# Three of four feed-forward layers of a diffusion backbone: two plain inner tiles in place of four, the gate halves of two more multiplied while the tokens arrive, and joins of fast products made in PSUM

## The chip, the cores and the metric

The kernel runs on one core of a Trainium2 chip. The metric is the device time in microseconds of one execution, the median of several runs. Times below are of that core.

## The reference, cut to what matters

One inference step of a small flow-matching backbone over 640 tokens (512 latent, 128 context) of width 1024. Two layers, each a half-step feed-forward, a token mixer and another half-step feed-forward, so six sub-layers n = 0 to 5: feed-forward at n = 0, 2, 3, 5, a Fourier mixer at n = 1, attention at n = 4.

```python
def _modulation(cond, w_mod, b_mod):
    m = jax.nn.silu(cond) @ w_mod + b_mod
    return m.reshape(cond.shape[0], N_MOD, D_MODEL)

def _swiglu(h, w1, w2):
    gate, up = jnp.split(h @ w1, 2, axis=-1)
    return (jax.nn.silu(gate) * up) @ w2

def _half_ffn(x, m, k, g_pre, g_post, w1, w2):
    h = _modulated_prenorm(x, g_pre, m, k)
    return x + 0.5 * m[:, 3 * k + 2, None] * _rmsnorm(_swiglu(h, w1, w2), g_post)
```

The inner width is 2816, that is 22 inner tiles f of 128. Everything is float32.

## The kernel before, in words

**Arithmetic.** A float32 operand is kept as two parts, hi (a copy on ScalarE in a shorter format, L220) and lo (the remainder, a subtraction on VectorE, L221). A product is three matmuls, hi·hi, hi·lo and lo·hi (`mm3`, L231, lines L234, L235, L236). The 640 tokens are two halves of 320 columns (five tiles of 128 tokens). A weight unit is 128 x 1024: a load of 512 KB into one of four raw buffers (`NRAW` L40, `raw_tile` L170), then its hi and lo. `unit(i)` (L175) sends units up to three ahead of the one that is multiplied; a raw buffer is free again when the last reader of what lies in it is done, and only then can the next load into it begin. Loads stand in one queue of SyncE, in program order.

**First matrix of a feed-forward (w1).** A plain inner tile multiplies gate and up for both halves: 2 x 2 x 8 x 3 = 96 matmuls of 128 x 320. A fast tile (`w1_fast`, L704) takes seven products of four chunks in place of eight, 84 matmuls, and joins them. It needs sums of weights (`send`, L182: gate, then on VectorE three sums at L195 to L197 from gate and up into a buffer `sums`, and a fourth at L203 for the last product, "all") and differences of token halves, made once per layer by `combine` (L666, subtractions at L692). Until those are ready the layer multiplies plain tiles: f = 0 to 3 are plain, 4 to 21 are fast, in each of the four layers. The joins of a fast tile are seven VectorE operations between PSUM banks and temporaries (L715, L718, L722, L728, L729, L733, L735) and three ScalarE ones. Its banks are x and y (kind `score`), z (kind `turn`, one bank) and w (kind `sum`, one bank). x takes the gate products, z and w take two products each, with a join between.

**Second matrix (w2).** After f = 4, 8, 12 and 16 (`SLICES`, L42) the hidden tiles made so far are multiplied with their rows of w2, for all five token tiles, in 512-column matmuls into the four `main` banks.

**Work put behind.** The modulation vectors of later sub-layers are matrix-vector products, done on VectorE: a job loads 512 KB of `w_mod_t` into a raw buffer and runs two SCALAR_TENSOR_TENSORs over it (`gemv`, L427, at L429). `BEHIND` (L44) and `behind` (L213) put nine jobs into each of the slices 0 to 3 of layers n = 0, 2 and 3, two into those of n = 5, and twelve into the Fourier mixer. Each engine runs its instructions in the order of the built program. In that order the nine jobs of a slice stand ahead of the weight sums of the next fast tile but one: after f = 4 and slice 0, the products of f = 5 find their sums ready, and those of f = 6 wait behind the jobs.

**Around it.** At the end of a layer each token tile is normalised and transposed for the next (`chain`, L564, a delay at L602 and transposes at L605). Gate vectors of the post-norm are transposed to rows by `gate_rows` (L531, a PE transpose at L538, its copy at L540), for n and, in layers 0 and 3, also for n + 1, right after each other before f = 20. `plan_ffn` (L819) writes the order of a layer out; the same plan serves all four.

Of the kernel before, what the change touches and what calls it, by code (L numbers as in the profile page):

```python
# [27 lines left out]
NF = DFF // P  # L28
# [14 lines left out]
FAST = range(4, NF)  # L43
# [83 lines left out]
class Kernel:  # L127
# [54 lines left out]
    def send(self, kind, src):  # L182

        nc, two, one = self.nc, slice(512, UNIT), slice(0, 512)
        at = slice(0, UNIT)
        if kind in ("plain", "block", "gate"):
            raw = self.raw_tile(src)  # L190
            self.fast["gate"] = raw
        elif kind == "sums":
            up, gate = self.raw_tile(src), self.fast["gate"]
            raw = self.raw.tile([P, UNIT], F32, tag="raw", name=self.name("sums"))
            nc.vector.tensor_tensor(raw[:, one], gate[:, one], up[:, one], op=ALU.add)  # L195
            nc.vector.tensor_tensor(up[:, one], up[:, one], up[:, two], op=ALU.add)
            nc.vector.tensor_tensor(raw[:, two], gate[:, one], up[:, one], op=ALU.add)  # L197
# [12 lines left out]
        self.split(hi, lo, raw[:, at])  # L210
        return hi, lo
# [352 lines left out]
    def chain(self, n, i, pss, acc=()):  # L564
# [36 lines left out]
        yield {0: 10500, 1: 14000, 2: 9200, 3: 11000, 4: 15000}[i]  # L601
# [19 lines left out]
    def ffn(self, layer, which, base, boundary):  # L621
# [3 lines left out]
        n = layer * 3 + 2 * which  # L625
        begun = [False, False]
# [7 lines left out]
        def w1(fs, half):  # L634
# [4 lines left out]
            if n == half == 0 and 0 in fs:  # L639
                rest, pss = self.begun  # L640
                for go in rest:
                    go()
            elif len(fs) == 1:
                for f in fs:
                    for j in range(2):
                        with self.behind_of(*[] if n or half else (*self.entered, self.load)):
                            w = self.unit(base + self.w1_at[f] + j)
                        with self.tc.issue_after(self.latest.ins):
                            pss.append(self.proj(w, lambda k: k * P, half, kind="score" if f == 2 and n == 0 else "main"))
            else:  # L650
                pss = self.multi([self.unit(base + self.w1_at[f] + j) for f in fs for j in range(2)], half,
                                 ("main", "main", "turn", "sum"))
# [45 lines left out]
        def product(f, ps, unit, at, x, start):  # L698
            w = self.unit(base + self.w1_at[f] + unit)
# [4 lines left out]
        def w1_fast(f):  # L704

            g[f] = self.ring(F32R).rearrange("p (a t) -> p a t", a=2)
            a, q = (self.temp("left")[:, :HALF] for _ in range(2))
            s, v = (self.temp("right")[:, :HALF] for _ in range(2))
            x, y, z = (self.bank(kind)[:, :HALF] for kind in ("score", "score", "turn"))
            product(f, x, 0, 0, lambda k: self.h.chunk(k, 0), True)  # L710
            with high():
                nc.scalar.activation(a, x, AF.Copy)
            product(f, y, 1, 512, lambda k: part(2, k), True)
            with high():
                tt(q, y, a, op=ALU.subtract)  # L715
            product(f, z, 1, 0, lambda k: part(3, k), True)
            with high():
                tt(a, q, z, op=ALU.subtract)  # L718
            w = self.bank("sum")[:, :HALF]
            product(f, w, 2, 0, lambda k: part(1, k), True)  # L720
            with high():
                tt(a, a, w, op=ALU.add)  # L722
            product(f, x, 0, 512, lambda k: self.h.chunk(4 + k, 0), False)
            with high():
                nc.scalar.activation(s, x, AF.Silu)
            product(f, z, 2, 512, lambda k: part(4, k), False)
# [4 lines left out]
            product(f, w, 3, 0, lambda k: self.h.chunk(4 + k, 1), False)  # L731
# [26 lines left out]
        def w2(s, tiles):  # L758
# [7 lines left out]
            for a0, f in [(a, f) for a in range(2) for f in range(f0, f1)] if ends else [(None, f) for f in range(f0, f1)]:  # L766
                w = self.unit(base + self.w2_at[s] + f - f0)
# [20 lines left out]
        for op, a, half in self.ffn_plan:  # L788
# [7 lines left out]
            elif op == "combine":  # L796
                combine(a)
            elif op == "fast":
                w1_fast(a)
# [19 lines left out]
    def plan_ffn(self):  # L819

        plan = []
        for half in (0, 1):
            for i, fs in enumerate(((0, 1), (2,), (3,))):
                plan += [("w1", fs, half)]
                if half:
                    plan += [("combine", step, None) for step in ((), (0, 1), (2, 3))[i]]
        due = 0
        for f in FAST:
            if f == NF - 2:
                plan += [("gates", None, None)]  # L830
            plan += [("fast", f, None)]
# [5 lines left out]
        self.ffn_plan = plan  # L837
        self.ffn_units, self.w1_at, self.w2_at = [], {}, {}
        for op, v, half in plan:
            if op == "fast":  # L840
                self.w1_at[v] = len(self.ffn_units)
                self.ffn_units += [("gate", v, 0), ("sums", v, 1)]
                self.ffn_units += [(kind, None, None) for kind in ("up", "all")]
            elif op == "w1":
                for f in v:
                    if f not in self.w1_at:
                        self.w1_at[f] = len(self.ffn_units)
                        self.ffn_units += [("w1", f, 0), ("w1", f, 1)]
            elif op == "w2" and v[0] not in self.w2_at:
                self.w2_at[v[0]] = len(self.ffn_units)  # L850
                f0, f1 = SLICES[v[0]]
                self.ffn_units += [("w2", f0, j) for j in range(f1 - f0)]

    def list_units(self):
        io = self.io
        self.plan_ffn()
        self.bases = []
        for i in range(DEPTH):
            for sub in range(3):
                self.bases.append(len(self.units))  # L860
                if sub != 1:
                    for op, v, j in self.ffn_units:
                        if op == "w2":
                            self.units.append(("plain", io["w2"][i, sub // 2, v + j]))
                        elif op == "w1":
                            self.units.append(("block" if v == 3 else "plain", io["w1"][i, sub // 2, v, j]))
                        else:
                            self.units.append((op, None if v is None else io["w1"][i, sub // 2, v, j]))
# [598 lines left out]
```

## Time and profile before

| | |
|---|---|
| median of 3 runs | 2233.11 us (2232.19 to 2233.71) |
| profiled execution | 2233.16 us, span 2231.4 us |
| granted TensorE clock in it | 0.996 |
| instructions in the span | 35240 |

The profile comes from one execution on the chip. A row of a group gives the line of the kernel, the engine, the operation, output and input by program name, the count, the busy time, the mean of one and the idle time before it with what ended it. A row of the timeline gives start, duration, engine, line, operation and, in brackets, the idle time before it and its releaser. In the timeline a duration is longer than the distance to the next start, since neighbours overlap by some tenths of a microsecond. In the view by windows each row is a stretch of time: busy time and count of PE, weight loads, VectorE, ScalarE and GpSimd, the granted clock (1.00 is full speed), the DMA share and GB/s.

### The profile page before, as it was taken

How to read it: one execution, taken by the hardware profiler on the slowest of the kernel's cores; microseconds unless marked ns; L12 is line 12 of the kernel's file. 1: busy time of each engine (PE TensorE's matmuls, PEld its weight loads, DVE VectorE, ACT ScalarE, POOL GpSimd, SP SyncE). 2: the span in 40 equal slices, each digit the busy share in tenths (PEclk: the TensorE clock that was granted, in tenths of full speed). 3: DMA queues.
4: the chain of work that ended last, by engine and by line, in shares of the span. 5: the costliest groups of instructions: out<-in, count | busy, mean ns of one | idle time of the engine just before them, and what ended most of it. 6: DMA issues, size and time to landing. Idle time of an engine off the chain costs nothing. (4 is left out here: it accounts for less than half of the span.)

```text
span 2231.4 us, 35240 instructions
## 1 busy us (share of the span) xinstructions
PE 2198.5 (99%) x13730; PEld 2051.7 (92%) x13730; DVE 1682.5 (75%) x3081; ACT 1155.6 (52%) x2186; POOL 43.7 (2%) x95
## 2 busy tenths in 40 slices
PE   7999999999999999999999999999999999999998
PEld 5999999999899999998999999989999899999997
DVE  5888898687868898887688898776555666766684
ACT  4544454464544454455444554466878644455452
POOL 0000000010000000001000000000000000000000
PEclk8999999999999999999999999999999999999999
DMA  8144444432413444444144344523343322322232
GB/s 313 67 142 161 140 143 144 178 127 94 167 72 123 139 146 149 154 143 178 57 143 150 133 147 150 195 77 105 108 118 111 106 74 95 114 87 88 101 123 104
DMA packets 84424, 288.13 MB, mean 129 GB/s; under 512 B 9537, under 2 KB 14497, under 8 KB 84129
## 3 DMA queue, kind: packets, MB, share of 16 engines
q1 hardware_dynamic: 83712, 285.23, 37.6%
q8 instruction: 107, 1.75, 0.3%
q10 hardware_dynamic: 544, 0.66, 0.1%
q14 instruction: 61, 0.49, 0.1%
HBM read 270.34 MB, written 11.58 MB: 126 GB/s over the span
## 5 line engine op out<-in xcount | busy, mean ns | idle before, releaser
L220 ACT ACTIVATE hi<-raw 128x1024 fp32r<-128x1024 f32 (+1 forms) x374 | 358.4, 973 | 330.2 <-PE score L235 86.9
L221 DVE TENSOR_TENSOR lo<-raw,hi 128x1024 fp32r<-128x1024 f32 (+1 forms) x374 | 416.0, 1118 | 142.1 <-ACT hi L220 140.9
L234 PE MATMUL main<-hi,ring 128*128 128x512 f32 (+2 forms) x1044 | 391.4, 375 | 0.0
L235 PE MATMUL main<-lo,ring 128*128 128x512 f32 (+2 forms) x1044 | 387.8, 372 | 0.8 <-DVE lo L221 0.8
L236 PE MATMUL main<-hi,ring 128*128 128x512 f32 (+2 forms) x1044 | 387.2, 371 | 0.0
L429 DVE SCALAR_TENSOR_TENSOR junk<-raw,wide 128x1024 bf16<-128x1024 f32 x256 | 313.1, 1223 | 95.7 <-DMA raw<-in_w_mod_t 91.3
L236 PE MATMUL score<-ring,lo 128*128 128x320 f32 x896 | 277.1, 309 | 0.3 <-DVE lo L221 0.3
L234 PE MATMUL score<-ring,hi 128*128 128x320 f32 x896 | 277.4, 310 | 0.0
L235 PE MATMUL score<-ring,hi 128*128 128x320 f32 x896 | 276.9, 309 | 0.0
L234 PEld LDWEIGHTS main<-hi,ring 128*128 128x128 f32 x1044 | 196.3, 188 | 34.9 <-issue 1.7
L235 PEld LDWEIGHTS main<-lo,ring 128*128 128x128 f32 x1044 | 196.3, 188 | 33.8 <-DVE lo L221 1.1
L236 PEld LDWEIGHTS main<-hi,ring 128*128 128x128 f32 x1044 | 196.1, 188 | 33.9 <-issue 0.2
L234 PE MATMUL turn<-ring,hi 128*128 128x320 f32 x648 | 200.5, 309 | 2.3 <-DVE left L718 2.1
L236 PE MATMUL sum<-ring,lo 128*128 128x320 f32 x648 | 200.2, 309 | 0.0
L235 PE MATMUL sum<-ring,hi 128*128 128x320 f32 x648 | 200.2, 309 | 0.0
L234 PE MATMUL sum<-ring,hi 128*128 128x320 f32 x648 | 200.2, 309 | 0.0
L235 PE MATMUL turn<-ring,hi 128*128 128x320 f32 x648 | 200.2, 309 | 0.0
L236 PE MATMUL turn<-ring,lo 128*128 128x320 f32 x648 | 200.2, 309 | 0.0
L781 ACT ACTIVATE y<-main 128x512 f32<-128x512 f32 x160 | 94.2, 591 | 200.0 <-PE main L236 199.0
L234 PE MATMUL main<-ring,hi 128*128 128x320 f32 x560 | 181.8, 325 | 1.6 <-ACT ring L220 1.6
L235 PE MATMUL main<-ring,hi 128*128 128x320 f32 x560 | 174.9, 312 | 0.8 <-DVE ring L221 0.8
L236 PE MATMUL main<-ring,lo 128*128 128x320 f32 x560 | 174.8, 312 | 0.0
(247 smaller groups left out, 4371.4 us busy)
## 6 DMA issues: line engine op xcount, KB each, us to landing
raw<-in_w SPq DMA_DIRECT2D x264, 512.0 KB, 3.9
raw<-in_w_mod_t SPq DMA_DIRECT2D x128, 512.0 KB, 3.5
raw<-in_qkv SPq DMA_DIRECT2D x26, 512.0 KB, 3.8
first<-in_w_mod_k SPq DMA_DIRECT2D x16, 512.0 KB, 8.8
spill<-ring SPq DMA_DIRECT2D x12, 640.0 KB, 2.9
ring<-spill SPq DMA_DIRECT2D x12, 640.0 KB, 7.2
raw<-in_bias SPq DMA_DIRECT2D x16, 448.0 KB, 3.8
raw<-in_four_in SPq DMA_DIRECT2D x8, 512.0 KB, 3.8
```

The costliest lines, as they stand in the source:

```text
L220: a = self.nc.scalar.activation(hi, src, AF.Copy)
L221: self.last_split = a, self.nc.vector.tensor_tensor(lo, src, hi.bitcast(F32), op=ALU.subtract)
L234: mm(out, whi, xhi, start=start, stop=False)
L235: mm(out, whi, xlo, start=False, stop=False)
L236: self.latest = mm(out, wlo, xhi, start=False, stop=stop)
L429: last = self.nc.vector.scalar_tensor_tensor(out=self.junk, in0=raw, scalar=1.0, in1=self.wide[:, cond, :], op0=ALU.mult, op1=ALU.mult, ac ...
L781: nc.scalar.activation(place(i, a), ps[a], AF.Copy)
```

## The change

The plan is made for each layer apart. Layer 0 keeps four plain tiles. In the layers 2, 3 and 5:

- Only f = 0 and 1 are plain. Half 0 of both is multiplied first, then `first_half` multiplies the gate product of half 0 for f = 2 and 3 into two `main` banks and puts a copy and the Silu of it away in a buffer. Then comes half 1 of f = 0, the four steps of `combine`, half 1 of f = 1. Fast tiles begin at f = 2. The gate and up units of f = 2 and 3 are loaded (in part again) for the sums: a load of 512 KB more for each, six in all.

In all four layers:

- The gate product of half 0 of tile f + 1 (`open_fast`) is multiplied within tile f, ahead of its second z product. So the gate unit of f + 1 is loaded within tile f, ahead of "all" of f; its raw buffer is kept until "all" of f + 1.
- 71 of the 78 fast tiles are "seeded": -x is copied by ScalarE into the y bank before y is multiplied on top of it, and y into the w bank. Three VectorE joins go (seven become four), and three ScalarE copies are added (three become six). The order is z, y; in the last two tiles y, z.
- The second call of `gate_rows` stands before f = 21, not right behind the first.
- The delay of token tile 4 in `chain` is 13000 in place of 15000.

Cut to its core, with new functions whole:

```diff
-FAST = range(4, NF)
+EARLY = 2
...
         if kind in ("plain", "block", "gate"):
             raw = self.raw_tile(src)
-            self.fast["gate"] = raw
-        elif kind == "sums":
-            up, gate = self.raw_tile(src), self.fast["gate"]
+            if kind == "gate":
+                self.fast["next"] = raw
+        elif kind in ("sums", "again"):
+            self.fast["gate"] = self.raw_tile(src[0]) if kind == "again" else self.fast.pop("next")
+            up, gate = self.raw_tile(src[1]), self.fast["gate"]
...
-        yield {0: 10500, 1: 14000, 2: 9200, 3: 11000, 4: 15000}[i]
+        yield {0: 10500, 1: 14000, 2: 9200, 3: 11000, 4: 13000}[i]
...
+        def first_half(fs):
+
+            room = self.ring(F32).rearrange("p (i t) -> p i t", t=HALF)
+            pss = [self.bank()[:, :HALF] for _ in fs]
+            stash.update({f: (room[:, 2 * i], room[:, 2 * i + 1]) for i, f in enumerate(fs)})
+            for i, f in enumerate(fs):
+                product(f, pss[i], "gate", 0, chunk(0, 0), True)
+                with high():
+                    copy(stash[f][0], pss[i], AF.Copy)
+            for i, f in enumerate(fs):
+                product(f, pss[i], "gate", 512, chunk(4, 0), False)
+                with high():
+                    copy(stash[f][1], pss[i], AF.Silu)
+
+        def open_fast(f):
+
+            if f is None or f in opened:
+                return
+            opened.append(f)
+            product(f, held["x"], "gate", 0, chunk(0, 0), True)
...
+            seeded = bool(opened)
...
+            steps = {
+                "y": lambda: product(f, y, "sums", 512, parts(2), not seeded),
+                "z": lambda: product(f, z, "sums", 0, parts(3), True),
+            }
+            if seeded:
+                with high():
+                    copy(y, x, AF.Copy, scale=-1.0)
+                a, q = left(), left()
+                for step in ("yz" if turned else "zy"):
+                    steps[step]()
+                    with high():
+                        if step == "z":
+                            copy(a, z, AF.Copy)
+                        else:
+                            w = self.bank("sum")[:, :HALF]
+                            copy(w, y, AF.Copy)
+                            copy(q, y, AF.Copy)
+                product(f, x, "gate", 512, chunk(4, 0), False)
+                s, v = right(), q
+                with high():
+                    copy(s, x, AF.Silu)
+                product(f, w, "up", 0, parts(1), False)
+                with high():
+                    tt(a, w, a, op=ALU.subtract)
...
+            open_fast(ahead)
+            product(f, z, "up", 512, parts(4), False)
...
-                nc.vector.scalar_tensor_tensor(out=q, in0=w, scalar=-1.0, in1=q, op0=ALU.mult, op1=ALU.subtract)
-                nc.scalar.activation(q, q, AF.Silu)
+                if seeded:
+                    q = left()
+                    copy(q, w, AF.Silu, scale=-1.0)
+                else:
+                    nc.vector.scalar_tensor_tensor(out=q, in0=w, scalar=-1.0, in1=q, op0=ALU.mult, op1=ALU.subtract)
+                    copy(q, q, AF.Silu)
...
                 self.gate_rows(n)
                 self.gates(n)
+            elif op == "rows":
                 if n % 3 == 0:
                     self.gate_rows(n + 1)
...
+            plan += [("w1", (0, 1), 0), ("first", (2, 3), None)]
+            plan += [("w1", (0,), 1)] + [("combine", step, None) for step in range(4)] + [("w1", (1,), 1)]
...
+        for f in range(early, NF):
+            turned = f >= NF - 2
+            if turned:
+                plan += [(("gates", "rows")[f - NF + 2], None, None)]
+            ahead = f + 1 if f + 1 < NF and (early == 4 or f > 2) else None
+            plan += [("fast", f, (ahead, turned))]
...
+            elif op == "fast":
+                again = early != 4 and v in (2, 3)
+                if not again:
+                    need(v, "gate")
+                need(v, "sums", "again" if again else "sums")
+                need(v, "up")
+                if half[0] is not None:
+                    need(half[0], "gate")
+                need(v, "all")
```

The lines of the changed kernel that the prediction speaks of: hi L222, lo L223, sums L197 to L199, "all" L205, the job's L431, mm3's L236 to L238, and the joins L765 (into a, from w), L793 and L794 (v from z), L804.

Three places show what moves. First the loads, SyncE, around slice 0 of layer 2 before; `in_w1` here are gate (raw_954) and up (raw_957) of f = 5, then the nine jobs, then the gate of f = 6:

```order
L172 DMA raw_937_6527<-in_w2 128x1024
L172 DMA raw_941_6560<-in_w2 128x1024
L172 DMA raw_944_6608<-in_w2 128x1024
L172 DMA raw_951_6635<-in_w2 128x1024
L172 DMA raw_954_6647<-in_w1 128x1024
L172 DMA raw_957_6659<-in_w1 128x1024
L172 DMA raw_963_6687<-in_w_mod_t 128x1024
L172 DMA raw_964_6717<-in_w_mod_t 128x1024
```

And in the changed kernel, where raw_905 is the gate of f = 5, raw_933 its up, raw_939 the gate of f = 6:

```order
L172 DMA raw_905_6480<-in_w1 128x1024
L172 DMA raw_916_6555<-in_w2 128x1024
L172 DMA raw_919_6574<-in_w2 128x1024
L172 DMA raw_922_6608<-in_w2 128x1024
L172 DMA raw_930_6635<-in_w2 128x1024
L172 DMA raw_933_6647<-in_w1 128x1024
L172 DMA raw_939_6673<-in_w1 128x1024
L172 DMA raw_942_6687<-in_w_mod_t 128x1024
L172 DMA raw_943_6717<-in_w_mod_t 128x1024
```

One load more, the gate of f = 6, stands ahead of the nine jobs and holds a buffer through the slice. The four raw buffers, called A to D, by their addresses in the built programs: before, gate, up and sums of f = 5 lie in D, A and C, and the nine jobs get B B C B C B C B A. After, gate, up and sums of f = 5 lie in C, A and D, the gate of f = 6 in B, and the nine jobs get D D D D A D C A D. The pattern (four in a row in one buffer) is the same in all twelve slices that have nine jobs.

Second, VectorE in the same slice. Before, its end: the last jobs, then the sums of f = 6 (L195 to L197) and their lo:

```order
L429 SCALAR_TENSOR_TENSOR junk_88,mod_82<-raw_971_6827,wide_79 128x1024
L715 TENSOR_TENSOR left_974_6833<-score_978_6837,left_973_6832 128x320
L449 SCALAR_TENSOR_TENSOR coef_83<-mod_82,vec_80 128x8 x2
L429 SCALAR_TENSOR_TENSOR junk_88,mod_82<-raw_971_6827,wide_79 128x1024
L718 TENSOR_TENSOR left_973_6832<-left_974_6833,turn_979_6838 128x320
L221 TENSOR_TENSOR lo_984_6860<-raw_982_6857,hi_983_6859 128x1024
L722 TENSOR_TENSOR left_973_6832<-left_973_6832,sum_985_6889 128x320
L195 TENSOR_TENSOR sums_987_6892<-raw_982_6857,raw_986_6890 128x512
L196 TENSOR_TENSOR raw_986_6890<-raw_986_6890 128x512
L197 TENSOR_TENSOR sums_987_6892<-raw_982_6857,raw_986_6890 128x512
L203 SCALAR_TENSOR_TENSOR raw_982_6857<-sums_987_6892,raw_982_6857 128x512
```

In the changed kernel, from the third job to the sixth (raw_946 is the fifth, in buffer A, which lo_938 sets free):

```order
L431 SCALAR_TENSOR_TENSOR junk_88,mod_82<-raw_944_6721,wide_79 128x1024 x2
L431 SCALAR_TENSOR_TENSOR junk_88,mod_82<-raw_945_6751,wide_79 128x1024
L223 TENSOR_TENSOR lo_938_6664<-raw_933_6647,hi_937_6663 128x1024
L223 TENSOR_TENSOR lo_941_6676<-raw_939_6673,hi_940_6675 128x1024
L431 SCALAR_TENSOR_TENSOR junk_88,mod_82<-raw_945_6751,wide_79 128x1024
L223 TENSOR_TENSOR lo_956_6838<-raw_905_6480,hi_955_6837 128x512
L431 SCALAR_TENSOR_TENSOR junk_88,mod_82<-raw_946_6755,wide_79 128x1024 x2
L431 SCALAR_TENSOR_TENSOR junk_88,mod_82<-raw_947_6785,wide_79 128x1024 x2
L765 TENSOR_TENSOR left_953_6834<-sum_957_6866,left_953_6834 128x320
```

Then its end, the ninth job, the sums of f = 6 (L197 to L199) and their lo:

```order
L431 SCALAR_TENSOR_TENSOR junk_88,mod_82<-raw_950_6827,wide_79 128x1024
L223 TENSOR_TENSOR ring_951_6831<-left_954_6835,ring_951_6831 128x320
L223 TENSOR_TENSOR ring_951_6831<-left_953_6834,ring_951_6831 128x320
L451 SCALAR_TENSOR_TENSOR coef_83<-mod_82,vec_80 128x8 x2
L431 SCALAR_TENSOR_TENSOR junk_88,mod_82<-raw_950_6827,wide_79 128x1024
L197 TENSOR_TENSOR sums_960_6885<-raw_939_6673,raw_959_6883 128x512
L198 TENSOR_TENSOR raw_959_6883<-raw_959_6883 128x512
L199 TENSOR_TENSOR sums_960_6885<-raw_939_6673,raw_959_6883 128x512
L205 SCALAR_TENSOR_TENSOR raw_939_6673<-sums_960_6885,raw_939_6673 128x512
L223 TENSOR_TENSOR lo_962_6890<-sums_960_6885,hi_961_6889 128x1024
```

In both kernels the sums stand behind the nine jobs; what has changed is which buffer each job waits for, and that all four VectorE joins of f = 5 now stand among the last jobs.

Third, PE at the passage from f = 5 to f = 6. Before, the last matmuls of the x product of f = 6 and the first of y, whose weights are the sums:

```order
L235 MATMUL score_997_6968<-ring_821_5702,hi_983_6859 128x320
L236 MATMUL score_997_6968<-ring_819_5700,lo_984_6860 128x320
L234 MATMUL score_998_6969<-ring_915_6416,hi_988_6896 128x320
L235 MATMUL score_998_6969<-ring_916_6417,hi_988_6896 128x320
L236 MATMUL score_998_6969<-ring_915_6416,lo_989_6897 128x320
```

In the changed kernel, where hi_940 and lo_941 are the gate of f = 6, and hi_961 and lo_962 its sums:

```order
L237 MATMUL score_874_6287<-ring_789_5670,hi_940_6675 128x320
L238 MATMUL score_874_6287<-ring_787_5668,lo_941_6676 128x320
L236 MATMUL turn_970_6962<-ring_865_6214,hi_961_6889 128x320
L237 MATMUL turn_970_6962<-ring_866_6215,hi_961_6889 128x320
L236 MATMUL score_875_6288<-ring_861_6201,hi_961_6889 128x320
L237 MATMUL score_875_6288<-ring_862_6202,hi_961_6889 128x320
L238 MATMUL turn_970_6962<-ring_865_6214,lo_962_6890 128x320
L236 MATMUL turn_970_6962<-ring_865_6214,hi_961_6889 128x320
```

Ahead of the first use of the sums stands one gate product of f = 6 of twelve matmuls in both kernels; behind it, z and y now need the sums one after another before anything else of f = 6 can run.

More of the change, by code (lines that the diff above doesn't have):

```diff
@@ L650, in w1 @@
             else:
-                pss = self.multi([self.unit(base + self.w1_at[f] + j) for f in fs for j in range(2)], half,
+                pss = self.multi([self.unit(base + w1_at[f, kind]) for f in fs for kind in ("gate", "up")], half,
                                  ("main", "main", "turn", "sum"))
@@ L702, in product @@
                 self.mm3(ps, w[0][:, a : a + P], w[1][:, a : a + P], *x(k), start and k == 0, k == 3, not start)
-        def w1_fast(f):
-            g[f] = self.ring(F32R).rearrange("p (a t) -> p a t", a=2)
[L707 to L726, printed above, removed]
@@ new lines, in ffn @@
+        chunk = lambda c, half: lambda k: self.h.chunk(c + k, half)
+        parts = lambda i: lambda k: part(i, k)
+        copy = nc.scalar.activation
+        stash, held, opened = {}, {}, []
+        def first_half(fs):
[10 more added lines that the diff above has]
+                    copy(stash[f][1], pss[i], AF.Silu)
@@ new lines, in open_fast, with w1_fast @@
+        def open_fast(f):
[3 more added lines that the diff above has]
+            product(f, held["x"], "gate", 0, chunk(0, 0), True)
+        def w1_fast(f, ahead, turned):
+            g[f] = self.ring(F32R).rearrange("p (a t) -> p a t", a=2)
+            if not held:
+                held.update({kind: self.bank("score")[:, :HALF] for kind in "xy"})
+            seeded = bool(opened)
+            x, y = held["x"], held["y"]
+            z = self.bank("turn")[:, :HALF]
+            left, right = (lambda kind=kind: self.temp(kind)[:, :HALF] for kind in ("left", "right"))
+            steps = {
[23 more added lines that the diff above has]
+            else:
+                if f in stash:
+                    b, s = stash.pop(f)
+                else:
+                    open_fast(f)
+                    b, s = left(), right()
+                    with high():
+                        copy(b, x, AF.Copy)
+                q = left()
+                steps["y"]()
+                with high():
+                    tt(q, y, b, op=ALU.subtract)
+                steps["z"]()
+                a, v = left(), right()
+                with high():
+                    tt(a, q, z, op=ALU.subtract)
+                w = self.bank("sum")[:, :HALF]
+                product(f, w, "up", 0, parts(1), True)
+                with high():
+                    tt(a, a, w, op=ALU.add)
+                if opened:
+                    product(f, x, "gate", 512, chunk(4, 0), False)
+                    with high():
+                        copy(s, x, AF.Silu)
+            open_fast(ahead)
+            product(f, z, "up", 512, parts(4), False)
@@ L787, in ffn @@
         turn = list(range(TILES))
-        for op, a, half in self.ffn_plan:
+        for op, a, half in plan:
             if op == "w2" and a[0] == end:
@@ L797, in ffn @@
                 combine(a)
+            elif op == "first":
+                first_half(a)
             elif op == "fast":
-                w1_fast(a)
+                w1_fast(a, *half)
             elif op == "w2":
@@ L817, in ffn, with plan_ffn @@
                     nc.sync.dma_start(out=self.xs[n + 1][c], in_=src.rearrange("p (c t) -> p c t", c=2))
[L819 removed]
+    def plan_ffn(self, n):
+        early = EARLY if n else 4
         plan = []
[L822 to L826, printed above, removed]
[L827 to L831 removed]
+        if early == 4:
+            for half in (0, 1):
+                for i, fs in enumerate(((0, 1), (2,), (3,))):
+                    plan += [("w1", fs, half)]
+                    if half:
+                        plan += [("combine", step, None) for step in ((), (0, 1), (2, 3))[i]]
+        else:
+            plan += [("w1", (0, 1), 0), ("first", (2, 3), None)]
+            plan += [("w1", (0,), 1)] + [("combine", step, None) for step in range(4)] + [("w1", (1,), 1)]
+        due = 0
+        for f in range(early, NF):
[4 more added lines that the diff above has]
+            plan += [("fast", f, (ahead, turned))]
             if f == SLICES[due][1]:
@@ L836, in plan_ffn, with need @@
         plan += [("w2", (due, tiles), None) for tiles in ((0, 1), (2,), (3, 4))]
-        self.ffn_plan = plan
-        self.ffn_units, self.w1_at, self.w2_at = [], {}, {}
-        for op, v, half in plan:
[L840 to L843, printed above, removed]
+        units, w1_at, w2_at = [], {}, {}
+        def need(f, kind, as_=None):
+            if (f, kind) not in w1_at:
+                w1_at[f, kind] = len(units)
+                units.append((as_ or kind, f, 0))
+        for op, v, half in plan:
+            if op == "first":
+                for f in v:
+                    need(f, "gate", "plain")
+            elif op == "fast":
[7 more added lines that the diff above has]
+                need(v, "all")
             elif op == "w1":
                 for f in v:
[L846 to L850, printed above, removed]
+                    for kind in ("gate", "up"):
+                        need(f, kind, "w1" if kind == "gate" else "w1up")
+            elif op == "w2" and v[0] not in w2_at:
+                w2_at[v[0]] = len(units)
                 f0, f1 = SLICES[v[0]]
-                self.ffn_units += [("w2", f0, j) for j in range(f1 - f0)]
+                units += [("w2", f0, j) for j in range(f1 - f0)]
+        return plan, units, w1_at, w2_at
     def list_units(self):
         io = self.io
-        self.plan_ffn()
         self.bases = []
+        self.plans = {}
         for i in range(DEPTH):
```

26 lines of the change are left out of this document (17 added, 9 removed).

## The prediction

> **What bounds the kernel now.** I read the busy shares first, then the waits, then one slice of the timeline.
>
> ```profile
> PE 2198.5 (99%) x13730; PEld 2051.7 (92%) x13730; DVE 1682.5 (75%) x3081; ACT 1155.6 (52%) x2186; POOL 43.7 (2%) x95
> ```
>
> TensorE (PE) is busy 99% of a span of 2231.4 us at a clock of 0.996. The time is the sum of its matmuls: fewer matmuls shorten it one for one, and any new wait of PE lengthens it one for one. Whether the change pays is thus a question of whether what feeds PE still comes in time. In the list of waits PE has hardly any; the long one that matters is on VectorE (DVE), the modulation jobs waiting for their loads:
>
> ```profile
> PE turn L538 <- ACT rms L540: 2.7, 2, 1.5
> PE turn L234 <- DVE left L718: 2.1, 2, 1.4
> DVE junk L429 <- DMA raw<-in_w_mod_t: 91.3, 54, 3.7
> raw<-in_w_mod_t SPq DMA_DIRECT2D x128, 512.0 KB, 3.5
> ```
>
> So the jobs already wait 91.3 us, and it costs PE nothing, as long as the chain behind them ends in time. How much time is left shows in one slice: layer 2, slice 0. By windows, w2 runs from 683.58 (call this W) for 27.23 us and fast tile f = 5 behind it for 12.31:
>
> ```profile
> 683.58:710.81 27.23, 27.23 (x123) 22.53 (x122) 20.78 (x35) 10.30 (x17) 0.00 (x0) 1.00 0.42 142
> 710.81:723.12 12.31, 12.31 (x85) 12.31 (x84) 12.17 (x24) 4.29 (x8) 0.00 (x0) 1.00 0.55 201
> ```
>
> The timeline of DVE over the same stretch, and PE at its end (from L197 to the lo of the sums ScalarE, ACT, makes their hi):
>
> ```profile
> 684.91 1.22 DVE L221 TENSOR_TENSOR lo<-sums,hi 128x1024 fp32r<-128x1024 f32 x1
> ...
> 686.85 1.22 DVE L429 SCALAR_TENSOR_TENSOR junk<-raw,wide 128x1024 bf16<-128x1024 f32 x1
> ...
> 693.14 1.23 DVE L429 SCALAR_TENSOR_TENSOR junk<-raw,wide 128x1024 bf16<-128x1024 f32 x1 [2.91 <-DMA raw<-in_w_mod_t]
> 694.41 1.22 DVE L429 SCALAR_TENSOR_TENSOR junk<-raw,wide 128x1024 bf16<-128x1024 f32 x1
> 695.67 1.23 DVE L429 SCALAR_TENSOR_TENSOR junk<-raw,wide 128x1024 bf16<-128x1024 f32 x1
> ...
> 700.29 1.23 DVE L429 SCALAR_TENSOR_TENSOR junk<-raw,wide 128x1024 bf16<-128x1024 f32 x1 [2.12 <-DMA raw<-in_w_mod_t]
> ...
> 718.50 0.48 DVE L718 TENSOR_TENSOR left<-left,turn 128x320 f32<-128x320 f32 x1
> 718.90 1.22 DVE L221 TENSOR_TENSOR lo<-raw,hi 128x1024 fp32r<-128x1024 f32 x1
> 720.03 0.48 DVE L722 TENSOR_TENSOR left<-left,sum 128x320 f32<-128x320 f32 x1
> 720.43 0.69 DVE L195 TENSOR_TENSOR sums<-raw,raw 128x512 f32<-128x512 f32 x1
> 721.15 0.69 DVE L196 TENSOR_TENSOR raw<-raw 128x512 f32<-128x512 f32 x1
> 721.88 0.69 DVE L197 TENSOR_TENSOR sums<-raw,raw 128x512 f32<-128x512 f32 x1
> ...
> 723.69 1.23 DVE L221 TENSOR_TENSOR lo<-sums,hi 128x1024 fp32r<-128x1024 f32 x1
> ```
>
> ```profile
> 724.88 0.31 PE L234 MATMUL score<-ring,hi 128*128 128x320 f32 x1
> 725.03 0.31 PE L235 MATMUL score<-ring,hi 128*128 128x320 f32 x1
> 725.17 0.31 PE L236 MATMUL score<-ring,lo 128*128 128x320 f32 x1
> ```
>
> The lo of the sums of f = 6 ends at 723.69 + 1.23 = 724.92, and PE reads it at 725.17, W + 41.6. Before, this chain (nine jobs, sums, hi, lo) is done 0.25 us ahead of its need. DVE is 75% busy on average, and yet here there is no room: that is the place to look at.
>
> **The change, part by part.**
>
> *Matmuls taken out.* The PE rows above start 0.147 us apart (724.88, 725.03, 725.17; 12.31 us over 84 matmuls gives 0.1466). Two tiles in each of three layers become fast, 96 - 84 = 12 matmuls less each: 72 x 0.1466 = 10.6 us less. Everything on PE is on the path, so this is a full gain.
>
> *PE's two waits.* The second `gate_rows` no longer finds the one `turn` bank held by the first one's copy: 2.7 us less; the wait for L718, two times 1.1 us, goes with the join of that line in seeded tiles: 2.1 less. I take both, 4.8, with 0 as the other end.
>
> *Jobs through one buffer.* In before the nine jobs of a slice use two buffers by turns; a load runs while DVE works on the other. Only the first two go through one buffer, and those rows give its price: 686.85 to 693.14 is 6.29. In the changed kernel the gate of f = 6 holds the other buffer through the slice, and four jobs go one after another through one. Two more places of before's trace show jobs through one buffer, the Fourier mixer and, with two jobs a slice, layer 5:
>
> ```profile
> 499.24 1.23 DVE L429 SCALAR_TENSOR_TENSOR junk<-raw,wide 128x1024 bf16<-128x1024 f32 x1 [3.68 <-DMA raw<-in_w_mod_t]
> 500.51 1.22 DVE L429 SCALAR_TENSOR_TENSOR junk<-raw,wide 128x1024 bf16<-128x1024 f32 x1
> ...
> 505.31 1.23 DVE L429 SCALAR_TENSOR_TENSOR junk<-raw,wide 128x1024 bf16<-128x1024 f32 x1 [3.37 <-DMA raw<-in_w_mod_t]
> ```
>
> ```profile
> 1868.90 1.22 DVE L429 SCALAR_TENSOR_TENSOR junk<-raw,wide 128x1024 bf16<-128x1024 f32 x1
> ...
> 1875.46 1.22 DVE L429 SCALAR_TENSOR_TENSOR junk<-raw,wide 128x1024 bf16<-128x1024 f32 x1 [3.18 <-DMA raw<-in_w_mod_t]
> ```
>
> The pair of a job takes 2 x 1.27 = 2.5 (499.24 to 500.51), the load 3.5: 6.07 from job to job in the mixer, which I use as 6.1 since nothing else of DVE's work comes between there. Now the slice of the changed kernel, from W, in DVE's order:
> - The first load waits for the lo of the sums of f = 5. That ended at W + 2.5 before (684.91 + 1.22); two more steps (L804, a lo, 0.4 each) and ScalarE's Silu stand ahead of it now: W + 3.4. The first job starts 3.5 later, at 6.9.
> - Jobs one to four start at 6.9, 13.0, 19.1, 25.2. Ahead of the fourth's second half stand two lo of 1.13. The first of these sets the fifth job's buffer free, at 25.2 + 1.27 + 1.13 = 27.6; its load lands 3.5 later, at 31.1.
> - From there the loads are ahead (two buffers and then three). DVE works through: five jobs at 2.53 are 12.7, and the joins L765, L793, L794, L804, two lo of 320 columns at 0.4 each and the mod and coef steps some 0.5: 2.9. It ends at 46.7.
> - Three sums at 0.72 (720.43, 721.15, 721.88): 48.9. ACT's hi, to where lo started before (721.88 + 0.69 to 723.69), 1.1: 50.0. lo 1.13: 51.1.
> - PE wants that lo at 27.23 + 12.31 + 12 x 0.147 (the second gate product of f = 6, the last work that is there) + 0.6 (the four matmuls that need hi only) = W + 41.9.
>
> So PE waits 51.1 - 41.9 = 9.2 us, once in each of the twelve slices: 110 us. Behind PE's wait nothing is left of f = 6 that could run; what stands queued behind DVE's waiting jobs (the joins of f = 5) is due before 46.7 and hides in the same wait. Bounds of the 9.2: the load issued at 695.67, when the second half of the second job was done with its buffer, was ready only at 700.29, 4.6 in place of 3.5; five loads so long make it 14. If the first load comes no later than before (3.3 in place of 6.9 for the first job) it is 5.6. Layer 5 has two jobs a slice, in one buffer before and after: no stall.
>
> *What a stall does to the clock.* The one place of this trace where PE shows a low clock is the start, while it waits for its first weights:
>
> ```profile
> 36.00:38.00 2.00, 2.00 (x10) 2.00 (x9) 0.00 (x0) 0.38 (x1) 0.00 (x0) 0.50 1.10 402
> 38.00:40.00 2.00, 2.00 (x9) 2.00 (x10) 1.33 (x6) 0.81 (x2) 0.00 (x0) 0.50 1.08 429
> 40.00:42.00 2.00, 2.00 (x12) 2.00 (x11) 1.30 (x3) 1.97 (x6) 0.00 (x0) 0.76 0.93 369
> ```
>
> PE works there at a granted clock of 0.50, up to a stretch of 0.76. From 36 to 42 the loss is 2 x (0.50 + 0.50 + 0.24) = 2.5 us. If every 9 us stall is followed by that, it is 12 x 2.5 = 30 us; ends 0 (the clock stays) and 3.0 each (0.50 for all six), 36 in all. I take 30. [...]
>
> *Entry of the layers 2, 3, 5.* The fast tiles begin two plain tiles earlier, so the combinations of token halves have less cover. In before, steps stand 0.735 apart:
>
> ```profile
> 648.33 0.82 DVE L692 TENSOR_TENSOR square<-y 128x640 f32<-128x640 f32 x1
> 649.06 0.82 DVE L692 TENSOR_TENSOR square<-square,y 128x640 f32<-128x640 f32 x1
> ```
>
> Eight subtractions and eight lo make 11.8 us, beside splits of weights; half 1 of two plain tiles covers 96 x 0.147 = 14.1. That is about even: I take 1 us a layer, 3 in all, with 0 and 6 as ends. Six loads more (3 MB) fall where SyncE's queue is not waited for.
>
> *Joins, the order z, y, and the delay.* DVE's work per fast tile falls by three joins at 0.40 (718.50 to 718.90), and ACT, busy 52%, takes three copies. In a stretch that DVE and ACT aren't the bound of, this is nothing. PE's z bank must be emptied by L793 within the twelve matmuls of "all" (1.76 us), where before the same step had 36 (5.3 us): nothing, as long as DVE isn't late; its price is a rival below. The delay of tile 4: nothing, since its transposes follow DVE's steps.
>
> Sum, from the profiled execution's own 2233.2 (1.8 outside its span; the median of three is 2233.1): 2233.2 - 10.6 - 4.8 + 110 + 30 + 3 = 2361 us.
>
> **The rivals.**
>
> *Faster: the buffers don't matter.* If the jobs end by W + 41.9 less 4.4 (sums, hi, lo) anyway, because loads land sooner than 3.5 or a buffer comes free earlier, only the gains stay: 2233.2 - 10.6 - 4.8 = 2218. For it: DVE has less other work. Against it: the chain would have to lose 9.2 us, and four loads of 3.5 one after another are 14 by themselves. It decides at a stall of 15.4/12 = 1.3 us a slice, where the gains are used up. 0.08.
>
> *Hardly changed: only the joins' cover.* No stall in the slices, but L793 comes after "all" in seeded tiles, by some 0.5 us each: 71 x 0.5 = 35 gives 2253; at 0.2 each it eats the gain, 2232. In the rows above a join (L718, L722) stands behind a step of 1.2 us now and then, so one half a step late is thinkable. 0.08, of which 0.03 end within 0.2% of before.
>
> *Slower, but the clock stays.* 2361 - 30 = 2331: one stretch at the start is little evidence for the ramp. It lies within my case, and in its range.
>
> **How the numbers follow.** The slices' stall, with or without the clock, has 0.84. Its own range: stalls of 5.6 without the ramp give 2218 + 67 = 2285; 14 with 36 of ramp, 2218 + 168 + 36 + 6 = 2428. Both ends at once are unlikely; 2300 to 2420 holds nearly all of this case, and the other two are outside. What a measurement can tell from no change is about 0.2%, 4.5 us: faster 0.08, same 0.03, slower 0.89.
>
> **What would show it.** Right: PE waits at L236 or L238 of `turn` for hi or lo of the sums, twelve times, near 9 us each, in layers 0, 2 and 3 and not in 5; DVE's wait for `in_w_mod_t` well above 91.3; a granted clock near 0.5 behind each wait, and a mean below 0.996; some 72 matmuls fewer. Wrong: PE still at 99% with no such wait; stalls in layer 5 too, or in every tile (then it is the joins); or stalls at the entries. If the stalls come at 4 us or less, the load's time or the first load's place was mis-sized.

## The result, and the profile after

The changed kernel takes 2354.93 us (median of 5, 2353.78 to 2357.53) against 2233.11 before: a ratio of 1.0547 (95% interval 1.0531 to 1.0562). The forecast was 2361. The profiled execution has a span of 2353.6, against 2231.4: 122.2 us more.

The busy shares of the changed kernel, and its waits of PE and DVE:

```profile
PE 2223.6 (94%) x13658; PEld 2067.4 (88%) x13658; DVE 1641.0 (70%) x2934; ACT 1239.7 (53%) x2417; POOL 43.6 (2%) x95
```

```profile
PE turn L236 <- ACT hi L222: 98.5, 12, 8.7
PE turn L333 <- DMA first<-in_w_mod_k: 12.7, 3, 9.7
PE score L1332 <- DVE col L1335: 2.4, 1, 2.4
```

```profile
DVE junk L431 <- DMA raw<-in_w_mod_t: 218.2, 74, 4.7
```

PE went from 99% to 94% busy, with 72 matmuls fewer (13730 to 13658). One row holds nearly all of it: twelve waits, 98.5 us, at the first z product of a tile, for the hi of the sums. Before, that row wasn't there. On DVE the jobs' wait for their loads rose from 91.3 to 218.2. That DVE waits more is no proof yet: it waited 91.3 before and cost nothing. The timeline of layer 2, slice 0 shows that the two waits are one chain. W, the first matmul of w2, is at 726.32 here. First DVE:

```profile
733.75 1.23 DVE L431 SCALAR_TENSOR_TENSOR junk<-raw,wide 128x1024 bf16<-128x1024 f32 x1 [3.21 <-DMA raw<-in_w_mod_t]
...
739.82 1.22 DVE L431 SCALAR_TENSOR_TENSOR junk<-raw,wide 128x1024 bf16<-128x1024 f32 x1 [3.57 <-DMA raw<-in_w_mod_t]
...
745.92 1.22 DVE L431 SCALAR_TENSOR_TENSOR junk<-raw,wide 128x1024 bf16<-128x1024 f32 x1 [3.60 <-DMA raw<-in_w_mod_t]
...
752.06 1.23 DVE L431 SCALAR_TENSOR_TENSOR junk<-raw,wide 128x1024 bf16<-128x1024 f32 x1 [3.65 <-DMA raw<-in_w_mod_t]
...
771.67 1.21 DVE L431 SCALAR_TENSOR_TENSOR junk<-raw,wide 128x1024 bf16<-128x1024 f32 x1
772.81 0.68 DVE L197 TENSOR_TENSOR sums<-raw,raw 128x512 f32<-128x512 f32 x1
773.53 0.69 DVE L198 TENSOR_TENSOR raw<-raw 128x512 f32<-128x512 f32 x1
774.25 0.69 DVE L199 TENSOR_TENSOR sums<-raw,raw 128x512 f32<-128x512 f32 x1
774.98 0.69 DVE L205 SCALAR_TENSOR_TENSOR raw<-sums,raw 128x512 f32<-128x512 f32 x1
776.07 1.22 DVE L223 TENSOR_TENSOR lo<-sums,hi 128x1024 fp32r<-128x1024 f32 x1 [0.40 <-ACT hi L222]
```

And PE, from the last gate product of f = 6 on:

```profile
767.47 0.31 PE L238 MATMUL score<-ring,lo 128*128 128x320 f32 x1
776.09 0.64 PE L236 MATMUL turn<-ring,hi 128*128 128x320 f32 x1 [8.31 <-ACT hi L222]
776.52 0.47 PE L237 MATMUL turn<-ring,hi 128*128 128x320 f32 x1
...
779.38 0.47 PE L236 MATMUL turn<-ring,hi 128*128 128x320 f32 x1
779.65 0.47 PE L237 MATMUL turn<-ring,hi 128*128 128x320 f32 x1
```

The first four jobs start 6.1 us apart (733.75, 739.82, 745.92, 752.06), each with 3.2 to 3.7 us of DVE idle ahead of it: one load, then one pair, through one buffer. Before, the jobs of this slice waited three times, 2.91, 2.12 and 1.14 us. The sums end at W + 48.6, their lo at W + 51.0; PE, with nothing left to do at 767.78, stands for 8.31. Then its matmuls start 0.27 apart, not 0.147. The windows around the wait show why in their clock column:

```profile
767.00:769.00 2.00, 0.78 (x6) 0.52 (x4) 2.00 (x6) 0.00 (x0) 0.00 (x0) 1.00 0.69 244
769.00:771.00 2.00, 0.00 (x0) 0.00 (x0) 2.00 (x7) 1.20 (x3) 0.00 (x0) 0.93 0.00 0
771.00:773.00 2.00, 0.00 (x0) 0.00 (x0) 2.00 (x7) 0.00 (x0) 0.00 (x0) 0.50 0.00 0
...
777.00:779.00 2.00, 2.00 (x8) 1.78 (x8) 2.00 (x3) 1.45 (x2) 0.00 (x0) 0.50 0.26 61
779.00:781.00 2.00, 2.00 (x10) 2.00 (x9) 1.18 (x3) 0.44 (x1) 0.00 (x0) 0.51 0.50 201
781.00:783.00 2.00, 2.00 (x14) 1.75 (x14) 1.93 (x3) 0.75 (x2) 0.00 (x0) 1.00 0.80 248
```

PE is granted half its clock from 771 to 781, five microseconds of them with work. The mean clock fell from 0.996 to 0.972.

The 122.2 add up: 98.5 of waits; PE's busy time up by 25.1, that is 35.7 by which matmuls were stretched less the 10.6 taken out; the other idle time down by 1.4.

### The profile page after: what moved, and what is told of

It reads as the page before. It is cut to its first block, busy times and chain, and to the rows that moved or that the text cites. A ratio compares the mean times of both kernels' runs of the same rounds, so it can differ in the third digit from the quotient of the medians.

```text
span 2353.6 us, 35207 instructions
## 1 busy us (share of the span) xinstructions
PE 2223.6 (94%) x13658; PEld 2067.4 (88%) x13658; DVE 1641.0 (70%) x2934; ACT 1239.7 (53%) x2417; POOL 43.6 (2%) x95
## 5 line engine op out<-in xcount | busy, mean ns | idle before, releaser
L223 DVE TENSOR_TENSOR lo<-raw,hi 128x1024 fp32r<-128x1024 f32 (+1 forms) x386 | 424.1, 1113 | 116.1 <-ACT hi L222 113.9
L431 DVE SCALAR_TENSOR_TENSOR junk<-raw,wide 128x1024 bf16<-128x1024 f32 x256 | 313.0, 1223 | 222.0 <-DMA raw<-in_w_mod_t 218.2
L222 ACT ACTIVATE hi<-raw 128x1024 fp32r<-128x1024 f32 (+1 forms) x386 | 369.8, 969 | 174.7 <-PE turn L237 76.3
L236 PE MATMUL main<-hi,ring 128*128 128x512 f32 (+2 forms) x1044 | 391.3, 375 | 0.0
L238 PE MATMUL main<-hi,ring 128*128 128x512 f32 (+2 forms) x1044 | 387.3, 371 | 0.0
L236 PE MATMUL turn<-ring,hi 128*128 128x320 f32 x672 | 218.1, 324 | 98.5 <-ACT hi L222 98.5
L236 PE MATMUL score<-ring,hi 128*128 128x320 f32 x920 | 288.7, 314 | 0.0
L237 PE MATMUL score<-ring,hi 128*128 128x320 f32 x920 | 287.6, 313 | 0.0
L238 PE MATMUL score<-ring,lo 128*128 128x320 f32 x920 | 286.5, 311 | 0.0
L236 PEld LDWEIGHTS main<-hi,ring 128*128 128x128 f32 x1044 | 196.3, 188 | 34.9 <-issue 1.7
L238 PEld LDWEIGHTS main<-hi,ring 128*128 128x128 f32 x1044 | 196.1, 188 | 33.8 <-issue 0.2
L236 PEld LDWEIGHTS turn<-ring,hi 128*128 128x128 f32 x672 | 132.3, 197 | 103.3 <-ACT hi L222 101.6
L238 PE MATMUL turn<-ring,lo 128*128 128x320 f32 x672 | 216.5, 322 | 0.0
L237 PE MATMUL turn<-ring,hi 128*128 128x320 f32 x672 | 214.8, 320 | 0.0
L236 PE MATMUL sum<-ring,hi 128*128 128x320 f32 x672 | 209.3, 311 | 1.2 <-DVE left L765 1.2
L237 PE MATMUL sum<-ring,hi 128*128 128x320 f32 x672 | 207.6, 309 | 0.0
L238 PE MATMUL sum<-ring,lo 128*128 128x320 f32 x672 | 207.6, 309 | 0.0
L236 PE MATMUL main<-ring,hi 128*128 128x320 f32 x560 | 182.3, 326 | 1.6 <-ACT ring L222 1.6
L236 PEld LDWEIGHTS score<-ring,hi 128*128 128x128 f32 x920 | 176.5, 192 | 0.4
```

Source lines behind the costliest of these rows:

```text
L222: a = self.nc.scalar.activation(hi, src, AF.Copy)
L223: self.last_split = a, self.nc.vector.tensor_tensor(lo, src, hi.bitcast(F32), op=ALU.subtract)
L236: mm(out, whi, xhi, start=start, stop=False)
L237: mm(out, whi, xlo, start=False, stop=False)
L238: self.latest = mm(out, wlo, xhi, start=False, stop=stop)
L431: last = self.nc.vector.scalar_tensor_tensor(out=self.junk, in0=raw, scalar=1.0, in1=self.wide[:, cond, :], op0=ALU.mult, op1=ALU.mult, ac ...
```

## The experiments

The theory: the next tile's gate, loaded early and held through a slice of w2, leaves the nine jobs one raw buffer. The main rival: the new joins, their order and the copies on ScalarE keep DVE behind. Times are medians; a ratio is against the kernel before on the same chip, with its 95% interval.

**No opening across a slice.**

```diff
-            ahead = f + 1 if f + 1 < NF and (early == 4 or f > 2) else None
+            ahead = f + 1 if f + 1 < NF and (early == 4 or f > 2) and f != SLICES[due][1] else None
...
             seeded = bool(opened)
+            if seeded:
+                open_fast(f)
```

> The changed kernel, but a fast tile's gate is not opened across a slice of w2: the tile ahead of each slice opens nothing, and the tile behind it opens its own x. Seeding, two plain tiles, first_half and everything else stay. The nine jobs of a slice then find two buffers by turns again. Buffer theory (the gate load held through the slice leaves the jobs one buffer): the twelve waits of 8.2 us (98.5 in all) and the clock's loss behind them (PE busy rose by 25.1 though 10.6 of matmuls went, so 35.7) both go: 2354.9 - 98.5 - 35.7 = 2221, some 12 under before. Rival, that the new order and the ScalarE copies of the seeded joins keep VectorE behind: waits stay, above 2330.

Measured: 2251.36, ratio 1.008 (1.0065 to 1.0095). The twelve long waits are gone, and the time falls by 104. But it stays 30 above the 2221 expected. Its waits of PE:

```profile
PE sum L236 <- ACT sum L759: 9.1, 12, 2.1
PE turn L236 <- ACT left L802: 5.0, 9, 0.6
PE turn L236 <- DVE left L795: 3.4, 4, 1.2
PE sum L236 <- DVE left L767: 3.0, 9, 0.5
```

These are joins that come late just behind the jobs: the seed of w on ACT, the last Silu, the emptying of z. So the buffer theory holds for the large part, and the rival can hold for a part of up to 30 that shows once the large one is gone. Some of it may be of this edit's own making: the run with five buffers, below, has the same joins, and the row for the seed of w (9.1 here) isn't in its list.

**Five raw buffers.**

```diff
-NRAW = 4
-NBLK = 20
+NRAW = 5
+NBLK = 19
```

> The changed kernel with five raw buffers in place of four; the room comes from 19 in place of 20 blocks of the ring. Nothing else. Buffer theory: the gate may stay held, since the jobs have a second buffer again: near 2221, plus whatever one ring block less costs (unknown, 0 to 10). Rival (order of VectorE and joins): no gain from a buffer, 2340 to 2360.

Measured: 2230.61, ratio 0.9988 (0.9979 to 0.9998). The gate is held as in the changed kernel and all jobs but the last half of one still stand in front of the sums; by the addresses in the built program they go to two buffers by turns. The stall is gone: the buffers decide, not the order. The jobs' wait for their loads falls from 218.2 to 51.5. Left of PE's new waits is the cover of the z bank, that is the time that L793 has to empty it:

```profile
DVE junk L431 <- DMA raw<-in_w_mod_t: 51.5, 86, 1.8
PE turn L236 <- DVE left L793: 6.5, 10, 1.4
```

**Jobs without loads.**

```diff
-                        self.gemv(self.raw_tile(self.io["w_mod_t"][layer, j]), layer, j)
+                        self.gemv(self.wide[:, 0, :], layer, j)
```

> The changed kernel, but each modulation job reads a tile that already lies in SBUF in place of its load from w_mod_t; the 256 vector operations stay, the 128 loads go, so the modulation vectors are not the reference's. Buffer theory: VectorE does the same work without the waits; the sums of the next tile are done at about W + 36 in place of 50, no stall: 2215 to 2222. Rival (VectorE has too much to do ahead of the sums): the same work stands ahead, so the twelve waits stay near 8 us: above 2330. Clock alone can't differ here.

Measured: 2222.76 in one run. PE has no wait for hi of the sums. The 256 vector operations are all there, but not all where they were: with no load to wait for they run earlier, and the last one starts at 819.59. In the four slices of layer 0 and in slices 0 and 1 of layer 2, 15 to 17 of the 18 operations of a slice still stand between the sums of one tile and the next; in the other six slices there are none. So only the first six slices test the rival. In slice 0 of layer 2, with 17 ahead, the sums end at W + 33.3 and their lo at W + 36.2. There DVE has time enough for the work; what it lacked was loads.

**Only the held buffer, in the kernel before.**

```diff
-            self.fast["gate"] = raw
+            if kind == "gate":
+                self.fast["next"] = raw
         elif kind == "sums":
+            self.fast["gate"] = self.fast.pop("next")
...
-            w = self.unit(base + self.w1_at[f] + unit)
+            w = self.unit(base + self.w1_at[f, unit])
...
             if op == "fast":
-                self.w1_at[v] = len(self.ffn_units)
-                self.ffn_units += [("gate", v, 0), ("sums", v, 1)]
-                self.ffn_units += [(kind, None, None) for kind in ("up", "all")]
+                for j, kind in enumerate(("gate", "sums", "up", "all")):
+                    if kind == "all" and v + 1 < NF:
+                        self.w1_at[v + 1, 0] = len(self.ffn_units)
+                        self.ffn_units.append(("gate", v + 1, 0))
+                    if (v, j) not in self.w1_at:
+                        self.w1_at[v, j] = len(self.ffn_units)
+                        self.ffn_units.append((kind, v if j < 2 else None, j))
```

> The kernel before with one thing of the change: the gate unit of the next fast tile is loaded and split ahead of the last product of this one, and so holds its raw buffer through the slice. All matmuls, joins and plain tiles are those of before. Buffer theory: four jobs through one buffer again, waits of 7 to 10 us in twelve slices and the ramp behind them: 2340 to 2380. Rival (the stall comes from the seeded joins or the z, y order): no stall, 2231 to 2240.

Measured: 2334.91 in one run, 5 below the range. With the matmuls and joins of before, and one load and its split put earlier:

```profile
PE score L236 <- ACT hi L222: 59.9, 12, 5.2
PE score L236 <- ACT left L714: 12.5, 12, 1.8
DVE junk L431 <- DMA raw<-in_w_mod_t: 175.2, 61, 5.1
```

Twelve waits for the sums again, 5.0 each and 1.0 more for the x bank just ahead, 6.0 in place of 7 to 10; PE's busy time is 33.3 above before's with the same 13730 matmuls. This run makes the stall out of nothing but the unit loaded early and the buffer that it holds. In the built program the first four jobs of each of the twelve slices again share one buffer. The last five go, in the letters used for the changed kernel, to A C D A C here and to A D C A D there; whether that is what makes the waits shorter wasn't tried.

**Useless work in place of the stall.**

```diff
                 a, q = left(), left()
+                if n < 5 and f - 2 in (4, 8, 12, 16):
+                    for _ in range(4):
+                        product(f, z, "gate", 0, chunk(0, 0), True)
```

> The changed kernel, with useless work in place of the stall: ahead of the first z product of f = 6, 10, 14 and 18 in the layers 0, 2 and 3, 48 more matmuls of 128 x 320 are put on PE (the gate product four times over into the z bank, written over afterwards). That is 12 x 48 x 0.147 = 84.5 us of work. Clock theory (a stall costs its own length and then the ramp, 35.7 in all): the ramp goes, some 2 us of wait stay each time (z's bank is free only when L793 is done, some 1.6 later): 2354.9 - 98.5 - 35.7 + 84.5 + 25 = 2330, faster though PE has more to do; mean clock back at 0.99. Rival (what PE's busy time gained behind the stalls isn't the clock): about 2354.9 - 98.5 + 84.5 + 25 = 2366.

Measured: 2341.6 (two runs), ratio to before 1.048 (1.046 to 1.0499). It is 13 faster than the changed kernel with 576 matmuls more, and its mean clock is 0.993. That is the clock theory's sign, but a third of the way from its number (2330) to the rival's (2366). The waits are as expected, the clock isn't: PE's busy time rose by 65.4 for 84.5 of work, so of the 35.7 of stretched time 19.1 went and 16.6 stayed. Its wait for the z bank in the list, and two places of it in the timeline, layer 2 slice 0 and layer 0 slice 3:

```profile
PE turn L236 <- DVE left L796: 22.8, 14, 2.2
```

```profile
409.68 0.42 PE L236 MATMUL turn<-ring,hi 128*128 128x320 f32 x1 [2.05 <-DVE left L796]
...
762.43 0.42 PE L236 MATMUL turn<-ring,hi 128*128 128x320 f32 x1 [2.05 <-DVE left L796]
```

And the windows behind each of the two:

```profile
409.00:411.00 2.00, 1.32 (x9) 1.32 (x10) 2.00 (x6) 0.00 (x0) 0.00 (x0) 1.00 0.73 248
411.00:413.00 2.00, 2.00 (x15) 2.00 (x14) 2.00 (x5) 0.87 (x2) 0.00 (x0) 1.00 0.02 8
...
762.00:764.00 2.00, 1.57 (x9) 1.57 (x10) 2.00 (x5) 0.05 (x1) 0.00 (x0) 0.85 0.60 238
764.00:766.00 2.00, 2.00 (x9) 2.00 (x8) 2.00 (x7) 0.83 (x2) 0.00 (x0) 0.50 0.00 0
766.00:768.00 2.00, 2.00 (x13) 2.00 (x12) 2.00 (x7) 0.00 (x0) 0.00 (x0) 0.80 0.00 0
```

After the second the clock fell, after the first it didn't; in all it fell in six of the twelve places, behind waits of 1.80 to 2.24 us. This run took only part of the ramp away: past the kernel's start, some 70 matmuls of 320 columns start about 0.267 apart, where the changed kernel has 156.

**The z bank's cover.** The order y, z for the second tile behind each slice, on top of five buffers.

```diff
-            plan += [("fast", f, (ahead, turned))]
+            plan += [("fast", f, (ahead, turned or f - 2 in (4, 8, 12, 16)))]
```

> The run with five raw buffers, and one thing more: the second fast tile behind each slice (f = 6, 10, 14, 18) takes the order y, z that the change gives only to the last two tiles, so that 24 matmuls and not 12 lie between its predecessor's second z product and its own first. The run with five buffers has ten waits of PE at the first z product for L793 (6.5 in all, and some PE rows drawn out by it). Theory that what is left over of the expected 2221 is this cover: 8 of the 2230.6 go, 2220 to 2225. Rival (the loss is the ring block given up, or spread): 2228 to 2232.

Measured: 2232.31, ratio 0.9994 (0.9985 to 1.0003): no gain, and the theory behind it falls. The wait moved:

```profile
PE score L236 <- ACT right L762: 6.1, 9, 1.3
PE sum L236 <- DVE left L765: 2.2, 3, 1.1
```

With z later, the Silu of x and the join into a are late instead. It isn't one bank's cover: what DVE and ACT owe the tile behind the jobs is late, by some 0.7 us on average in these rows, whichever product comes first.

**Control: before with five buffers,** nothing else.

```diff
-NRAW = 4
-NBLK = 20
+NRAW = 5
+NBLK = 19
```

> A control: the kernel before with five raw buffers and 19 ring blocks, nothing else. Buffer theory: before had enough buffers, so none gains; the block given up costs little: 2231 to 2238. Rival (a fifth buffer is a gain of its own, and the run with five buffers says nothing about the change): 2222 to 2228.

Measured: 2226.56, ratio 0.9966 (0.9954 to 0.9978). A fifth buffer is a gain of its own, 6.6 us, and the ring block costs nothing that shows. My expectation was wrong. The list of its waits has neither of before's two rows that the prediction prices (2.7 for L540, 2.1 for L718); these 4.8 are most of the 6.6. How the buffer takes them away wasn't followed. So before was not just in time but in places a little late, and the changed kernel with five buffers is 4 slower than its own control, not 3 faster than before.

**Joins alone,** on top of five buffers.

```diff
-EARLY = 2
+EARLY = 4
```

> The run with five raw buffers, with four plain tiles in the layers 2, 3 and 5 as before and no first_half: the joins, the opening and the split gate rows alone, without the stall. By the count of matmuls it is 72 x 0.147 = 10.6 slower than the run with five buffers, less what the entries of three layers cost there (3 taken, 0 to 6): 2235 to 2241. Rival (two plain tiles fewer bring nothing, since the entry stalls eat it): 2229 to 2232.

Measured: 2246.17, ratio 1.005 (1.0034 to 1.0065). Against the control, 19.6 slower: opening ahead and seeded joins lose time here even with buffers enough. Against the changed kernel with five buffers, 15.6 slower, where 10.6 is the matmuls. Of the other 5, up to 1.7 is the clock: it fell to half once, from 150.81 to 154.22, behind a wait of 1.96 for L793 that the other run has at 1.38 and without a fall. The rest was not followed up.

**Only the two plain tiles,** with four and with five buffers:

```diff
-            seeded = bool(opened)
+            seeded = False
...
-            ahead = f + 1 if f + 1 < NF and (early == 4 or f > 2) else None
+            ahead = None
```

> Only the part of the change that takes matmuls out, with four raw buffers: two plain tiles and first_half in the layers 2, 3 and 5, the second gate rows before f = 21; no tile is opened ahead and none is seeded, so the joins and the order of products are those of before, no gate is held through a slice and the jobs have two buffers by turns. By the prediction's terms: 2233.2 - 10.6 (matmuls) - 2.7 (gate rows) + 3 (entries) = 2223, 2217 to 2226. Rival (the entries of three layers eat the gain, so that the early joins were needed): 2230 or more. The pair with and without two plain tiles at five buffers differed by 15.6, which would give 2216.

> The same with five raw buffers and 19 ring blocks. Before with five buffers was 2226.6; less 10.6 and 2.7, plus 0 to 3 for the entries: 2213 to 2216, or 2211 by the pair that differed by 15.6. It should beat the kernel before, the changed one, and every run so far. Rival (the two gains overlap): no faster than the one with four buffers.

Measured: 2221.16 with four buffers, ratio 0.9945 (0.9931 to 0.9958); 2217.19 with five, ratio 0.9927 (0.9915 to 0.994). Both beat before and the changed kernel. Less work on PE pays as counted: 12 us against 10.3 by the prediction's terms. The second is 1 above its expected range. The two gains overlap in part: the buffer gives 4.0 here and 6.6 before, which differ by about the 2.7 of the gate rows' wait that either takes away. The busy shares of the faster one:

```profile
PE 2188.1 (99%) x13658; PEld 2041.6 (92%) x13658; DVE 1719.0 (78%) x3147; ACT 1172.4 (53%) x2204; POOL 43.4 (2%) x95
```

## Why the prediction was right, point by point

- *Matmuls taken out, 10.6:* right. PE has 72 fewer, and two plain tiles alone gave 12 with the gate rows.
- *PE's two waits, 4.8:* right as rows, since both are gone, but new short waits took most of it back: the idle time outside the twelve waits fell by 1.4 only.
- *Jobs through one buffer, 9.2 in twelve slices:* right, in place and in size. The chain was forecast to end its jobs at W + 46.7, its sums at 48.9, its lo at 51.1, and ended at 46.6, 48.6 and 51.0. The waits are in layers 0, 2 and 3 and not in 5. The profile shows 8.2 each and not 9.2, as the wait ends with hi; what is missing for lo lies between the first matmuls behind it. That the buffer is the cause is shown from four sides: give a buffer back, take the loads away (in six slices), drop the opening, and make the stall in before. One bound was mis-added: five loads longer by 1.1 make 14.7, not 14, which lifts the far end of the range by some 8 and changes nothing here.
- *The clock, 30:* the size is about right. Busy time was stretched by 35.7. Of this at least 18.7 is plain low clock: 189 matmuls of 320 columns start about 0.267 apart, 33 of them in the kernel's first 45 us, where before has all its 28; the other 156 x 0.12 are 18.7 (three of them stand behind the wait of 2.4 at L1332). Most of the rest lies at the first matmuls behind a wait (0.43 apart at 776.09), where a low clock and a missing lo come together; I did not part them. An upper end is in the clock records: behind the twelve stalls PE's rows cover 55.5 us of half clock, and half of that is 27.7. My 2.5 us a stall, from the kernel's start, was more than either.
- *Entries, 3:* not seen apart. Two plain tiles alone came out 2 below their sum, so it is nearer 0.
- *Joins and z cover, nothing:* wrong in the small. Hidden behind the stall are some 13 us (2230.6 against 2217.2, two plain tiles) to 20 us (2246.2 against 2226.6, four) that show once it is gone. The rival "only the joins' cover" had the right mechanism beside the main one, at 13 to 20 us and not 35, and not at z alone.
- *The rival "faster":* false, by its own condition: the jobs would have had to end by W + 37.5, and ended at W + 46.6, since DVE stood 3.57 to 3.65 ahead of each of the jobs two to four.

The sum came out near (2361 against 2355) with errors on both sides: the clock 6 short, entries and waits off by some 3 each, the stall 12 long by the listed waits.

## What to carry to other kernels

A load put earlier may cost nothing on its queue and yet takes a buffer for as long as its data are needed: 2354.93 us with four buffers, 2230.61 with five and the same loads. So ask who else draws from that pool in the meantime, and count loads in flight before and after. A chain on an engine that is 75% busy can still be just in time: read the slack from one stage, lo done at 724.92 and read at 725.17, not from the average. And look for the part of a change that takes work off the bound engine and try it alone: two plain tiles gained 12 us while the parts meant to smooth the flow lost 134.

## What the runs showed of the hardware that was not expected

Half the granted clock came behind waits of PE of only 1.80 to 2.24 us, in six of twelve places of the run with useless work, and not always: of the two waits of 2.05 shown there, one was followed by 0.50 from 764 to 766, the other by 1.00 from 409 to 413. What parts the two was not shown; no run was made to test it.
